# Gates and branch outputs of a hybrid decoder trunk as tokens x 512 channels, with the merged sums transposed

## The chip, the cores and the metric

The kernel runs on one core of a Trainium2 chip. A core has a matrix engine (TensorE, in the rows PE, its weight loads PEld), a vector engine (VectorE, DVE), an activation engine (ScalarE, ACT), a general engine (GpSimd, POOL) and a queue engine (SyncE, SP) that issues the DMAs. The metric is the device time of one execution in microseconds, the median of three runs.

## The reference

Two layers run over 256 tokens of 1024 channels; each ends in a residual addition, and a last RMS norm follows. In a layer the normalised input `h` is projected to everything at once: queries, keys, values and gate logits of three attention branches (8 heads of 64 each, so 512 channels), an indexer, and 3 x 1024 merge logits.

```python
    oa = moba_attention(rope(qa), rope(ka), va).reshape(B, S, WIDTH) * jax.nn.silu(ga)
    ob = dsa_attention(rope(qb), rope(kb_), vb_, qi, ki, wi).reshape(B, S, WIDTH) * jax.nn.silu(gb)
    oc = forgetting_attention(qc, kc, vc, log_f).reshape(B, S, WIDTH) * jax.nn.silu(gc)
    y = jnp.einsum('nbsw,nwd->bsnd', jnp.stack([oa, ob, oc], axis=0), w_branch)
    gates = jax.nn.sigmoid(merge_logit).reshape(B, S, N_BRANCH, D_MODEL)
    merged = jnp.sum(gates * y, axis=2)
    return x + jnp.einsum('bsd,de->bse', merged, w_out)
```

With 256 tokens the first branch is plain causal attention. The second keeps, for each token, the 64 keys with the highest indexer score. The third adds a running sum of log forget gates to its scores.

## The kernel before, in words

All products are float32 to nearly full precision, made of three matmuls in the rounded type float32r: each operand is split into a high part (a rounded copy, made by ACT) and a low part (the difference, made by DVE), and high x high, high x low and low x high are added up. So a stage of 8 blocks of 128 input channels has 24 matmuls for each output tile.

Weights come by DMA in chunks into three `raw` buffers, and pieces of 128 x 1024 numbers are split into the rings `wh` and `wl` (6 slots each): ACT's copy at line 380 and DVE's subtraction at line 384. Activations stand transposed, channels on partitions: `hTh` and `hTl` are the parts of the normalised input, `og` those of the gated branch outputs.

There are two kinds of projection. `unit_b` loads 128 columns of weights into PE and streams all 256 tokens past them, so that its matmuls are 256 columns wide and its result is channels x tokens. `unit_a` loads 128 tokens and streams 512 weight columns, so that its result is tokens x 512 channels; values and the output projection use it. Both issue their matmuls at line 428 into one of three PSUM tiles `proj`.

Before the change the merge gates (`unit_m`, 8 blocks of 128 channels for each branch, two neighbours sharing the pieces) and the branch outputs (`unit_y`, likewise) are made as channels x tokens. ACT takes a tanh of the gate logits (line 900 into `acc` for branch 0, line 903 into `mth` for the others). DVE multiplies tanh plus one with the branch output (lines 929 and 934) and adds the second and third product to `acc` (line 936). The sums are then in the form that the output projection loads as its tokens, and `split_to` writes their two parts into the value buffers `V`, which are free by then (lines 418 and 419).

A planner written in the file sets the order of instructions. Operations are recorded with their costs by engine, dependences, buffers and a key (the number of the unit that they belong to); `Plan.run` then picks, again and again, the engine that can start soonest and on it the operation that can start first, the lower key among equals. Every engine runs its list in order. The units are numbered in the order in which the layer's code makes them: values, indexer and the first mixer with gates in between (`between`), the third branch's mixer with branch outputs, the second branch's mixer with branch outputs, then the last gates and branch outputs, then the output projection. A mixer makes query, key and gate of two pairs of heads at a time, and their attention (`attend`) has the key of the last key unit plus one. `select`, the choice of the 64 keys, is recorded behind the last indexer unit: eight rounds of the eight highest scores (lines 886 and 887) on DVE, with keys that grow by 2.

Of the kernel before, what the change touches and what calls it, by code (L numbers as in the profile page):

```python
# [15 lines left out]
S = 256  # L16
# [27 lines left out]
MTH = 8  # L44
NC1 = 8
DMA_KEY = (-95, -94, -85, -84)
HI_KEY = (-60, -48, -47, -46)
NB1 = 0
# [199 lines left out]
def hybrid_trunk(ctx, tc, x, norm_gain, w_in, forget_bias, w_branch, w_out, final_gain, consts, out):  # L248
# [71 lines left out]
    acc = pool.tile([128, KC, S], F32, name="acc")  # L320
# [21 lines left out]
    k_acc = [Tok() for _ in range(KC)]  # L342
# [113 lines left out]
    def unit_a2(name, gets, ah, al, ra):  # L456

        us = [unit(f"{name}{t}") for t in range(2)]
        ps = [Buf("proj") for _ in range(2)]
        for t, q in ((0, (0, 1, 2)), (1, (0, 1, 2)), (0, (3,)), (1, (3,))):  # L460
            unit_a(f"{name}{t}", gets, t, ah, al, ra, part=(us[t], ps[t], q))
        return list(zip(us, ps))

    def unit_a(name, gets, t, ah, al, ra, c=0, n=512, part=None):
        u, ps, q = part or (unit(name), Buf("proj"), range(4))
        o = lambda: T(ps)[:, :n].rearrange("p (b a) -> p b a", a=2)
        for i in q:
# [82 lines left out]
    def final_part(t, c, n, i, key, on_dve):  # L550

        a = acc.rearrange("p k c -> p (k c)")
        x, sq = xs[t][:, c:c + n], a[:, D + c:D + c + n]
# [8 lines left out]
        dve(lambda: DVE.tensor_tensor(x, x, a[:, c:c + n], op=ALU.mult), n, [k_fg], [kx], key + 0.5, "final",  # L562
# [333 lines left out]
    def unit_m(l, n, j, gates):  # L896
        c0 = COL["mg"] + n * D + (j // 2) * 256
        u, ps = unit_b(f"m{n}{j}", lambda k: win_b(l, c0, k), j % 2)
        if n == 0:
            act(lambda: ACT.activation(acc[:, j], T(ps)[:, :S], AF.Tanh, scale=0.5), S, True, [ps], [k_acc[j]], u, "mth")  # L900
            return
        th = gates[n, j] = Buf("mth")
        act(lambda: ACT.activation(T(th), T(ps)[:, :S], AF.Tanh, scale=0.5), S, True, [ps], [th], u, "mth")

    def merged(j):
        v = V[j // 4].rearrange("p t h c -> p (t h c)")
        i = j % 4
        return [v[:, (2 * i + p) * S:(2 * i + p + 1) * S] for p in range(2)]

    k_mg = [k_V[j // 4][j % 4] for j in range(KC)]  # L910

    def unit_y(l, n, j, oi, gates, rank):
        u = unit(f"y{n}{j}")
        p = wbr(l, n, j, u)
        ps = Buf("proj")
        gh, gl = og[oi]
        cs = slice((j % 2) * 128, (j % 2) * 128 + 128)
        o = lambda: T(ps)[:, :S].rearrange("p (b a) -> p b a", a=2)
        g = []
        for k in range(4):  # L920
            wh, wl = lambda k=k: p[0].v[:, k, cs], lambda k=k: p[1].v[:, k, cs]
            g += [(wh, lambda k=k: turns(gh[:, k]), [p[0], k_og[oi][0][k]]), (wh, lambda k=k: turns(gl[:, k]), [p[0], k_og[oi][1][k]]),
                  (wl, lambda k=k: turns(gh[:, k]), [p[1], k_og[oi][0][k]])]
        g = [g[i] for i in (0, 1, 3, 4, 2, 5, 6, 7, 9, 10, 8, 11)]
        for a in (0, 6):
            mm_ops(o, g[a:a + 6], t_mm(256), [ps], u, f"y{n}{j}", a == 0, a == 6, True)
        ac = acc[:, j]
        if rank == 0:
            dve(lambda: DVE.scalar_tensor_tensor(ac, ac, 1.0, T(ps)[:, :S], op0=ALU.add, op1=ALU.mult), S,
                [ps], [k_acc[j]], u, "y")  # L930
            return
        th = gates[n, j]
        t = th
        dve(lambda: DVE.scalar_tensor_tensor(T(t), T(t), 1.0, T(ps)[:, :S], op0=ALU.add, op1=ALU.mult), S,
            [ps], [t], u, "y")
        plan.op([("DVE", t_dve(S), lambda: DVE.tensor_tensor(ac, ac, T(t), op=ALU.add)),
                 ("POOL", t_pool(S), lambda: POOL.tensor_tensor(ac, ac, T(t), op=ALU.add))], [t], [k_acc[j]], u, 0.0, "y").port = True
        if rank == 2:
            h, lo = merged(j)
            kh, kl = k_mg[j]  # L940
            split_to(lambda: plain(h), lambda: plain(lo), lambda: tiles(ac), S, False, [k_acc[j]], kh, kl, u, 0.5, "mg")
# [32 lines left out]
    hA = (lambda k, t: hTh[:, k, t * 128:(t + 1) * 128], lambda k, t: hTl[:, k, t * 128:(t + 1) * 128])  # L974
    mA = (lambda k, t: merged(k)[0][:, t * 128:(t + 1) * 128], lambda k, t: merged(k)[1][:, t * 128:(t + 1) * 128])

    def v_units(l, m, vi):
        gets = [lambda k, i=i: rows_a("A", w_in, l, COL["v" + m], i, k) for i in range(4)]
        for t in range(2):
            ra = [lambda k, p=p, t=t: [k_hT[p][t][k]] for p in range(2)]  # L980
            u, ps = unit_a(f"v{m}{t}", gets, t, hA[0], hA[1], ra)
            v_out(ps, t, vi, [ps], u)
# [62 lines left out]
    def m_of(l, n, gates, js):  # L1045
        return [lambda j=j: unit_m(l, n, j, gates) for j in js]

    def y_of(l, n, oi, rank, gates, js):
        return [lambda j=j: unit_y(l, n, j, oi, gates, rank) for j in js]
# [12 lines left out]

    def alternate(a, b):
        r = []
        for i in range(0, max(len(a), len(b)), 2):
            r += a[i:i + 2] + b[i:i + 2]
# [5 lines left out]
    for l in range(L):  # L1072
# [15 lines left out]
        for f in between(first, m_of(l, 0, gates, range(8)) + m_of(l, 2, gates, range(NC1))):  # L1088
            f()
        v_units(l, "c", 1)  # L1090
        for f in between(mixer(l, "c", 1, 1), alternate(m_of(l, 2, gates, range(NC1, 8)), y_of(l, 0, 0, 0, gates, range(8)))):
            f()
        v_units(l, "b", 0)
        for f in between(mixer(l, "b", 0, 0), alternate(y_of(l, 2, 1, 1, gates, range(8)), m_of(l, 1, gates, range(NB1)))):
# [53 lines left out]
```

## Time and profile before

| What | Value |
|---|---|
| Median of 3 runs | 602.46 us (602.02 to 602.86) |
| Profiled execution | 602.07 us |
| Its span, first to last instruction | 600.3 us |
| PE, DVE, ACT busy | 590.1, 526.0, 386.1 us |
| Mean granted TensorE clock | 0.997 of the upper level, 2.4 GHz |
| Moved by DMA | 107.69 MB, 179 GB/s |

Busy times of one engine are unions of its instructions' spans. Matmuls overlap, so two starts tell how long one occupies PE, and its recorded length does not. A releaser is the instruction that ended a wait, as semaphores tell.

### The profile page before, as it was taken

To read this page: it belongs to the slowest core of one execution; us is meant where nothing else is said; L and a number is where in the kernel's file an instruction comes from. 1 tells how busy PE (TensorE), PEld (TensorE's weight loads), DVE (VectorE), ACT (ScalarE), POOL (GpSimd) and SP (SyncE) were. 2 spreads that over 40 slices of the span, in tenths; PEclk is the share of its full clock that TensorE was granted. 3 is DMA by queue.
4 is the path that set the end of the run, shared out by engine and by line. 5 is a ranking of instruction groups with operands and counts; after the bars stand their busy time and mean duration, and the time that the engine had idled before them with its cause. 6 is when DMAs were issued, how large, how long until landed. Compare 5 with 4: busy or idle time off the path is not lost.

```text
span 600.3 us, 13137 instructions
## 1 busy us (share of the span) xinstructions
PE 590.1 (98%) x5164; PEld 568.9 (95%) x5164; DVE 526.0 (88%) x1232; ACT 386.1 (64%) x758; POOL 91.2 (15%) x100
## 2 busy tenths in 40 slices
PE   9999999999999999999999999999999999999995
PEld 8999999999999999999889999999999999999985
DVE  6799999986998999969588899998889989998783
ACT  5785575775767666765587566746766674776541
POOL 1234102200000504000003221230000014310001
PEclk9999999999999999999999999999999999999998
DMA  8859264836572654465546854465565455535701
GB/s 288 276 173 321 73 211 125 296 111 213 170 246 73 211 176 141 141 213 210 162 144 208 261 162 140 143 214 190 164 207 188 130 176 174 176 94 193 278 36 70
DMA packets 94461, 107.69 MB, mean 179 GB/s; under 512 B 4400, under 2 KB 82496, under 8 KB 94400
## 3 DMA queue, kind: packets, MB, share of 16 engines
q1 hardware_dynamic: 94112, 106.47, 55.4%
q8 instruction: 40, 0.66, 0.4%
q10 hardware_dynamic: 288, 0.39, 0.2%
q14 instruction: 21, 0.17, 0.1%
HBM read 105.79 MB, written 1.06 MB: 178 GB/s over the span
## 4 chain that ended last, share of the span: by engine, by line
PE 71%; DVE 24%; issue 3%; ACT 2%; POOL 0%; POOLq 0%; ACTq 0%
PE proj L428 62%; DVE wl L384 9%; PE d L609 2%; PE proj L1023 2%; DVE isc L887 2%; DVE e L683 1%; DVE t L886 1%; DVE rsh L483 1%; PE d L620 1%; DVE ptl L713 1%; DVE e L697 1%; DVE isc L865 1%; PE d L948 1%; ACT wh L380 1%; DVE rr L485 1%
## 5 line engine op out<-in xcount | busy, mean ns | idle before, releaser
L384 DVE TENSOR_TENSOR wl<-raw,wh 128x1024 fp32r<-128x1024 f32 (+1 forms) x190 | 240.3, 1282 | 27.5 <-ACT wh L380 22.6
L428 PE MATMUL proj<-hTh,wh 128*128 128x256 f32 (+1 forms) x1040 | 247.1, 277 | 0.0
L428 PE MATMUL proj<-hTl,wh 128*128 128x256 f32 (+1 forms) x1040 | 245.8, 276 | 0.0
L380 ACT ACTIVATE wh<-raw 128x1024 fp32r<-128x1024 f32 (+1 forms) x190 | 197.6, 1054 | 72.9 <-PE proj L428 40.2
L428 PEld LDWEIGHTS proj<-hTh,wh 128*128 128x128 f32 (+1 forms) x1040 | 199.0, 191 | 0.9
L428 PEld LDWEIGHTS proj<-hTl,wh 128*128 128x128 f32 (+1 forms) x1040 | 199.4, 192 | 0.2
L428 PE MATMUL proj<-hTh,wl 128*128 128x256 f32 (+1 forms) x1040 | 160.5, 277 | 0.6 <-DVE wl L384 0.6
L428 PEld LDWEIGHTS proj<-hTh,wl 128*128 128x128 f32 (+1 forms) x1040 | 136.8, 191 | 1.7 <-DVE wl L384 0.8
L484 POOL TENSOR_TENSOR rsh<-rsh,cst 128x256 f32<-128x256 f32 (+1 forms) x42 | 36.3, 866 | 314.8 <-DVE rsh L483 309.5
L687 ACT ACTIVATE e<-e,st 128x128 f32<-128x128 f32 x96 | 42.3, 442 | 17.7 <-DVE st L683 17.7
L486 POOL TENSOR_TENSOR rr<-rr,rsh 128x256 f32<-128x256 f32 (+1 forms) x42 | 46.7, 1116 | 10.1 <-DVE rr L485 5.6
L428 PE MATMUL proj<-wh,v 128*128 128x512 f32 (+1 forms) x144 | 33.7, 357 | 0.0
L428 PE MATMUL proj<-og0l,wh 128*128 128x256 f32 x128 | 31.9, 276 | 0.0
L428 PE MATMUL proj<-og0h,wh 128*128 128x256 f32 x128 | 31.9, 275 | 0.0
L428 PE MATMUL proj<-wh,hTl 128*128 128x512 f32 x80 | 30.6, 383 | 0.2 <-DVE hTl L546 0.2
L428 PE MATMUL proj<-wh,hTh 128*128 128x512 f32 x80 | 30.8, 385 | 0.0
L712 ACT ACTIVATE pth<-d 128x768 fp32r<-128x768 f32 x24 | 19.3, 803 | 17.0 <-PE o L726 15.0
L713 DVE TENSOR_TENSOR ptl<-d,pth 128x768 fp32r<-128x768 f32 x24 | 22.9, 952 | 7.7 <-ACT pth L712 7.6
L428 PEld LDWEIGHTS proj<-wh,v 128*128 128x128 f32 x144 | 25.3, 190 | 2.9
L428 PE MATMUL proj<-og0h,wl 128*128 128x256 f32 x128 | 24.8, 275 | 0.0
L428 PEld LDWEIGHTS proj<-og0l,wh 128*128 128x128 f32 x128 | 24.6, 192 | 0.0
L428 PEld LDWEIGHTS proj<-og0h,wh 128*128 128x128 f32 x128 | 24.6, 192 | 0.0
(190 smaller groups left out, 942.3 us busy)
## 6 DMA issues: line engine op xcount, KB each, us to landing
raw<-in_w_in_dram SPq DMA_DIRECT2D x74, 1024.0 KB, 5.3
raw<-in_w_branch_dram SPq DMA_DIRECT2D x24, 512.0 KB, 3.9
raw<-in_w_out_dram SPq DMA_DIRECT2D x8, 1024.0 KB, 5.8
brow<-drow SPq DMA_DIRECT2D x4, 512.0 KB, 6.5
raw<-in_w_in_dram SPq DMA_DIRECT2D x3, 512.0 KB, 6.4
x<-in_x_dram SPq DMA_DIRECT2D x4, 256.0 KB, 5.8
raw<-in_w_in_dram SPq DMA_DIRECT2D x2, 320.0 KB, 6.0
out_dram<-tmp SPq DMA_DIRECT2D x2, 320.0 KB, 2.5
```

The source lines that it names most:

```text
L380: ACT.activation(p[0].v, sel(c.v), AF.Copy)
L384: DVE.tensor_tensor(p[1].v, sel(c.v), p[0].v.bitcast(F32), op=ALU.subtract)
L428: PE.matmul(o(), a(), b(), start=first and i == 0, stop=last and i == n - 1)
L483: dve(lambda: DVE.stream_shuffle(T(sh)[:np_], a(), SWAP), S, [ps], [sh], key, "rope", t_dve(S) + 6.0)
L484: gps(lambda: POOL.tensor_tensor(T(sh)[:np_], T(sh)[:np_], s[:np_], op=ALU.mult), S, [k_rope], [sh], key, "rope")
L486: gps(lambda: POOL.tensor_tensor(T(r)[:np_], T(r)[:np_], T(sh)[:np_], op=ALU.add), S, [sh], [r], key, "rope")
L609: PE.matmul(T(d)[:, c:c + n].rearrange("p (b a) -> p b a", a=2), st[r, sl], turns(mv[r, :n]), start=i == 0, stop=i == 2, skip_group_check= ...
L687: act(lambda t=t, a=a, n=n, e=e, st=st: ACT.activation(T(e)[:, a:a + n], T(e)[:, a:a + n], AF.Exp, bias=T(st)[:, t:t + 1], scale=-1.0, acc ...
L712: act(lambda src=src, dst=dst: ACT.activation(dst(ph), src(), AF.Copy), 128 * n, True, [ps], k[:1], key, "pT", touch=[ph] + ps.banks)
L713: dve(lambda src=src, dst=dst: DVE.tensor_tensor(dst(pl), src(), dst(ph).bitcast(F32), op=ALU.subtract), 128 * n, [ps, k[0]], k[1:], key, ...
L887: dve(lambda o=o, t8=t8: DVE.match_replace(o, T(t8), o, TAKEN), n, [t8], [k_isc[i]], key + r * step, "top8")
L1023: PE.matmul(T(ps[t]).rearrange("p (b a) -> p b a", a=2), h(2 * i + x, t), turns(v3(w)[:, x]), start=left[t][0] == 23, stop=left[t][0] == 0)
```

## The change

Gates and branch outputs become units of the second kind: tokens x 512 channels, with one half of the channels (`hh`) and both token tiles in one unit, whose pieces of weights serve both tiles in turn. `unit_a2` takes the order of (token tile, pieces) as a list. Tanh, multiply and add work on 512 columns. The merged sums are then tokens x channels and have to be turned for the output projection: four transposes on PE for each half and token tile, from `acc` into a `d` tile of PSUM, from which ACT writes the high part and DVE the low part. The last branch's additions go to DVE alone; the others may go to POOL. Branch matrices are loaded in chunks of 512 columns. A mixer makes query, gate, key in this order, `select` begins 17 unit numbers later, and `between` hands out its units singly.

```diff
-MTH = 8
-NC1 = 8
+MTH = 4
+HC = (0, 1)
+O_ORDER = ((0, (0, 1)), (1, (0, 1)), (0, (2, 3)), (1, (2, 3)))
+M_ORDER = ((0, (0, 1)), (1, (0, 1)), (0, (2, 3)), (1, (2, 3)))
...
-    def wbr(l, n, j, k):
-        src = w_branch[l][n][:, (j // 2) * 256:(j // 2 + 1) * 256].rearrange("(k p) c -> p k c", p=128)
-        return piece(("Y", l, n, j // 2), ("Y", l, n, j // 2), src, [4, 256], lambda r: r, [4, 256], k)
+    def wbr(l, n, hh, i, k):
+        src = w_branch[l][n][:, hh * 512:(hh + 1) * 512].rearrange("(k p) c -> p k c", p=128)
+        return piece(("Y", l, n, hh, i), ("Y", l, n, hh), src, [4, 512], lambda r: r[:, 2 * i:2 * i + 2, :], [2, 512], k)
...
+    def unit_a2(name, gets, ah, al, ra, order, same=False):
+
+        n = len(gets)
         us = [unit(f"{name}{t}") for t in range(2)]
+        if n == 4:
+            unit(name)
         ps = [Buf("proj") for _ in range(2)]
-        for t, q in ((0, (0, 1, 2)), (1, (0, 1, 2)), (0, (3,)), (1, (3,))):
-            unit_a(f"{name}{t}", gets, t, ah, al, ra, part=(us[t], ps[t], q))
+        for t, q in order:
+            unit_a(f"{name}{t}", gets, t, ah, al, ra, part=(us[0] if same else us[t], ps[t], q))
         return list(zip(us, ps))
...
+    def units_m(l, n, hh, gates):
+        gets = [lambda k, i=i: rows_a("M", w_in, l, COL["mg"] + n * D + hh * W, i, k) for i in range(4)]
+        for t, (u, ps) in enumerate(unit_a2(f"m{n}{hh}", gets, hA[0], hA[1], rH, M_ORDER)):
+            if n == 0:
+                v, k = (lambda t=t: acc[:, t, hh * W:(hh + 1) * W]), k_acc[hh][t]
+            else:
+                k = gates[n, hh, t] = Buf("mth")
+                v = lambda k=k: T(k)
+            act(lambda v=v, ps=ps: ACT.activation(plain(v()), tiles(T(ps)), AF.Tanh, scale=0.5), W, True, [ps], [k], u, "mth")
...
+    def units_y(l, n, hh, oi, gates, rank):
...
+        for t, (u, ps) in enumerate(unit_a2(f"y{n}{hh}", gets, gA[0], gA[1], rG, ((0, (0, 1)), (1, (0, 1))))):
+            ac, ka = acc[:, t, hh * W:(hh + 1) * W], k_acc[hh][t]
+            if rank == 0:
+                dve(lambda ac=ac, ps=ps: DVE.scalar_tensor_tensor(plain(ac), plain(ac), 1.0, tiles(T(ps)), op0=ALU.add, op1=ALU.mult), W,
+                    [ps], [ka], u, "y")
+                continue
+            th = gates[n, hh, t]
+            dve(lambda th=th, ps=ps: DVE.scalar_tensor_tensor(plain(T(th)), plain(T(th)), 1.0, tiles(T(ps)), op0=ALU.add, op1=ALU.mult), W,
+                [ps], [th], u, "y")
+            ways = [("DVE", t_dve(W), lambda ac=ac, th=th: DVE.tensor_tensor(ac, ac, T(th), op=ALU.add)),
+                    ("POOL", t_pool(W), lambda ac=ac, th=th: POOL.tensor_tensor(ac, ac, T(th), op=ALU.add))]
+            plan.op(ways[:1] if rank == 2 else ways, [th], [ka], u, 0.0, "y").port = True
+            if rank < 2:
+                continue
+            at, kt = [d, d.banks[t]], Tok()
+
+            def tr(ac=ac, t=t, d=d):
+                for j in range(4):
+                    PE.transpose(T(d)[:, t * 512 + j * 128:t * 512 + (j + 1) * 128], ac[:, j * 128:(j + 1) * 128], ident)
+            pe(tr, 480.0, [ka, k_id], [kt], u, "mgT", MARGIN, touch=at)
...
+            act(lambda h=h, src=src: ACT.activation(h, src(), AF.Copy, scale=0.5), W, True, [kt], wh, u, "mg", touch=at)
+            dve(lambda h=h, lo=lo, src=src: DVE.scalar_tensor_tensor(lo, src(), 0.5, h.bitcast(F32), op0=ALU.mult, op1=ALU.subtract), W,
+                [kt] + wh, wl, u, "mg", t_dve(W) + 10.0, touch=at)
...
-                for hf in range(2) for kind in "qkg" for p in (2 * hf, 2 * hf + 1)]
+                for hf in range(2) for kind in "qgk" for p in (2 * hf, 2 * hf + 1)]
...
-                select(u + 3, 2.0)
+                select(u + 20, 2.0)
```

At the end of the first layer, on PE, the branch outputs of the last branch (from `og0h`) run into the output projection (from `v0` and `v1`, where the merged sums stand). Before:

```order
L428 MATMUL proj1_165<-og0h_95,wh4_67 128x256
L428 MATMUL proj1_165<-og0l_96,wh4_67 128x256
L428 MATMUL proj1_165<-og0h_95,wh4_67 128x256
L428 MATMUL proj1_165<-og0l_96,wh4_67 128x256
L428 MATMUL proj1_165<-og0h_95,wl4_74 128x256 x2
L428 MATMUL proj0_164<-wh5_68,v0_84 128x512 x4
L428 MATMUL proj0_164<-wl5_75,v0_84 128x512 x2
L428 MATMUL proj0_164<-wh0_63,v0_84 128x512 x4
L428 MATMUL proj0_164<-wl0_70,v0_84 128x512 x2
L428 MATMUL proj0_164<-wh1_64,v1_85 128x512 x4
```

Now, at the same place, from the second transpose of the layer on (line 941 turns `acc` into `d`):

```order
L941 MATMUL d1_164<-cst_109,acc_114 128x128 x4
L429 MATMUL proj1_161<-wh4_67,og0h_95 128x512
L429 MATMUL proj1_161<-wh4_67,og0l_96 128x512
L429 MATMUL proj1_161<-wh4_67,og0h_95 128x512
L429 MATMUL proj1_161<-wh4_67,og0l_96 128x512
L429 MATMUL proj1_161<-wl4_74,og0h_95 128x512 x2
L941 MATMUL d0_163<-cst_109,acc_114 128x128 x4
L429 MATMUL proj2_162<-wh5_68,v0_84 128x512 x4
L429 MATMUL proj2_162<-wl5_75,v0_84 128x512 x2
L429 MATMUL proj2_162<-wh0_63,v0_84 128x512 x4
L429 MATMUL proj2_162<-wl0_70,v0_84 128x512 x2
L429 MATMUL proj0_160<-wh5_68,v0_84 128x512 x4
```

Blocks of four transposes stand between the matmuls now, and the wide matmuls take the outputs as their loaded side.

On DVE at the same place, the multiplies (`mth` with `proj`), adds (`acc`), splits of merged sums (`v0`) and weight subtractions (`wl`). Before:

```order
L934 SCALAR_TENSOR_TENSOR mth0_156<-mth0_156,proj2_166 128x256
L936 TENSOR_TENSOR acc_114<-acc_114,mth0_156 128x256
L934 SCALAR_TENSOR_TENSOR mth1_157<-mth1_157,proj1_165 128x256
L936 TENSOR_TENSOR acc_114<-acc_114,mth1_157 128x256
L384 TENSOR_TENSOR wl1_71<-raw1_124,wh1_64 128x1024
L419 SCALAR_TENSOR_TENSOR v0_84<-acc_114,v0_84 128x256 x2
```

Now, from the first multiply of the last branch on:

```order
L930 SCALAR_TENSOR_TENSOR mth0_156<-mth0_156,proj1_161 128x512
L932 TENSOR_TENSOR acc_114<-acc_114,mth0_156 128x512
L385 TENSOR_TENSOR wl1_71<-raw1_124,wh1_64 128x1024
L930 SCALAR_TENSOR_TENSOR mth1_157<-mth1_157,proj2_162 128x512
L385 TENSOR_TENSOR wl2_72<-raw1_124,wh2_65 128x1024
L947 SCALAR_TENSOR_TENSOR v0_84<-d1_164,v0_84 128x4x128
L932 TENSOR_TENSOR acc_114<-acc_114,mth1_157 128x512
L930 SCALAR_TENSOR_TENSOR mth2_158<-mth2_158,proj0_160 128x512
```

The split reads the transposed sums from `d1`, and two weight subtractions and a split now stand ahead of the second add.

On DVE in the first layer's first mixer, the rounds of the selection (MAX and MATCH_REPLACE on `isc`), the low parts of the keys (`k1l`, `k2l`) and the weights. Before:

```order
L886 MAX t80_152<-isc_115 128x8
L886 MAX t81_153<-isc_115 128x8
L887 MATCH_REPLACE isc_115<-t80_152,isc_115 128x128
L887 MATCH_REPLACE isc_115<-t81_153,isc_115 128x256
L886 MAX t82_154<-isc_115 128x8
L886 MAX t83_155<-isc_115 128x8
L415 TENSOR_TENSOR k1l_102<-rr1_129,k1h_101 128x256
L415 TENSOR_TENSOR k2l_104<-rr0_128,k2h_103 128x256
L384 TENSOR_TENSOR wl3_73<-raw2_125,wh3_66 128x1024
```

Now, around the same two keys:

```order
L385 TENSOR_TENSOR wl3_73<-raw2_125,wh3_66 128x1024
L488 STREAM_SHUFFLE rsh0_126<-proj1_161 128x256
L416 TENSOR_TENSOR k1l_102<-rr1_129,k1h_101 128x256
L490 TENSOR_TENSOR rr0_128<-proj1_161,cst_109 128x256
L890 MAX t83_155<-isc_115 128x8
L894 TENSOR_SCALAR selb_116<-isc_115 128x128
L891 MATCH_REPLACE isc_115<-t83_155,isc_115 128x256
```

Weights and a key's rotation stand between the selection's rounds, whose last one comes behind the first key's low part.

## Rows read from the trace of the kernel before

**Rows 1.** The page: span and busy times.

```profile
span 600.3 us, 13137 instructions
PE 590.1 (98%) x5164; PEld 568.9 (95%) x5164; DVE 526.0 (88%) x1232; ACT 386.1 (64%) x758; POOL 91.2 (15%) x100
```

**Rows 2.** The timeline of PE from 300 to 319 us: start, length, instruction. Rows with a count hold several merged instructions; between the first two rows from 310.65 lie twelve matmuls, as between the next two and the last two.

```profile
300.36 1.04 PE L532 MATMUL d<-cst,tmp 128*128 128x128 f32 x8
301.15 0.46 PE L428 MATMUL proj<-wh,v 128*128 128x512 f32 x1
...
310.65 0.38 PE L428 MATMUL proj<-wh,hTh 128*128 128x512 f32 x1
...
313.24 0.38 PE L428 MATMUL proj<-wh,hTh 128*128 128x512 f32 x1
...
314.53 0.27 PE L428 MATMUL proj<-hTh,wh 128*80 128x256 f32 x1
...
315.84 0.27 PE L428 MATMUL proj<-hTh,wh 128*80 128x256 f32 x1
...
317.15 0.28 PE L428 MATMUL proj<-hTh,wh 128*128 128x256 f32 x1
...
318.49 0.28 PE L428 MATMUL proj<-hTh,wh 128*128 128x256 f32 x1
```

**Rows 3.** The waits of PE over the whole span: who waited for whom, us in total, times, longest. The rows left out are those of the program's start and of the normalisation between the layers.

```profile
PE o L725 <- DVE ot L743: 0.9, 2, 0.4
PE proj L428 <- DVE wl L384: 0.6, 1, 0.6
PE d L609 <- DVE k1l L415: 0.5, 1, 0.5
...
PE o L727 <- DVE ptl L713: 0.2, 1, 0.2
```

**Rows 4.** The timeline of PE at the five waits of the steady part, each time the instruction before the wait and the one behind it, with its idle time and releaser in brackets.

```profile
72.55 0.28 PE L609 MATMUL d<-k1h,ql 64*128 64x256 f32 x2
73.36 0.38 PE L609 MATMUL d<-k1l,qh 64*128 64x256 f32 x2 [0.54 <-DVE k1l L415]
...
91.79 0.22 PE L726 MATMUL o<-pth,v 128*128 128x128 f32 x1
92.25 0.27 PE L727 MATMUL o<-ptl,v 128*64 128x128 f32 x1 [0.24 <-DVE ptl L713]
...
233.03 0.39 PE L428 MATMUL proj<-og1h,wl 128*128 128x256 f32 x2
233.83 0.35 PE L725 MATMUL o<-pth,v 128*128 128x256 f32 x1 [0.41 <-DVE ot L743]
...
391.22 0.28 PE L428 MATMUL proj<-hTl,wh 128*128 128x256 f32 x1
392.14 0.71 PE L428 MATMUL proj<-hTh,wl 128*128 128x256 f32 x4 [0.65 <-DVE wl L384]
...
525.01 0.39 PE L428 MATMUL proj<-og1h,wl 128*128 128x256 f32 x2
525.84 0.35 PE L725 MATMUL o<-pth,v 128*128 128x256 f32 x1 [0.45 <-DVE ot L743]
```

**Rows 5.** Stretches of the span: from and to, length, busy time (and instructions) of PE, PEld, DVE, ACT and POOL, granted clock, busy share of the DMA engines, GB/s.

```profile
22.00:93.00 71.00, 70.23 (x668) 68.86 (x667) 68.09 (x182) 48.97 (x95) 19.78 (x20) 1.00 0.63 201
...
214.00:258.00 44.00, 43.59 (x445) 42.68 (x444) 43.45 (x117) 32.37 (x72) 8.52 (x9) 1.00 0.54 169
258.00:298.00 40.00, 40.00 (x287) 37.91 (x287) 29.29 (x46) 21.52 (x34) 0.00 (x0) 1.00 0.63 206
...
506.00:550.00 44.00, 43.55 (x444) 42.64 (x444) 43.24 (x116) 32.38 (x72) 8.53 (x9) 1.00 0.54 168
550.00:589.00 39.00, 39.00 (x284) 37.10 (x284) 27.61 (x45) 19.63 (x32) 0.00 (x0) 1.00 0.38 136
```

**Rows 6.** Transposes of 128 x 128 in the trace of before: a piece of the chain of waits (start, us, what), and the group of all 32 by line and shape (busy us, mean ns of one, idle before).

```profile
14.91 0.44 PE d L532 x4
...
L532 PE MATMUL d<-cst,tmp 128*128 128x128 f32 x32 | 4.3, 273 | 0.0
```

**Rows 7.** Groups of instructions by line and shape: engine, operation, operands, count, busy us, mean ns of one, idle time before them and what ended it.

```profile
L384 DVE TENSOR_TENSOR wl<-raw,wh 128x1024 fp32r<-128x1024 f32 x188 | 238.8, 1287 | 27.5 <-ACT wh L380 22.6 <-ACT tmp L854 2.2 <-PE proj L428 0.5
L486 POOL TENSOR_TENSOR rr<-rr,rsh 128x256 f32<-128x256 f32 x40 | 45.3, 1136 | 9.9 <-DVE rr L485 5.6 <-ACT wh L380 2.0
L934 DVE SCALAR_TENSOR_TENSOR mth<-mth,proj 128x256 f32<-128x256 f32 x32 | 12.9, 414 | 0.3 <-PE proj L428 0.2
L936 DVE TENSOR_TENSOR acc<-acc,mth 128x256 f32<-128x256 f32 x32 | 12.8, 422 | 0.2
L903 ACT ACTIVATE mth<-proj 128x256 f32<-128x256 f32 x32 | 12.0, 374 | 6.0 <-PE proj L428 5.9
L418 ACT ACTIVATE v<-acc 128x256 fp32r<-128x256 f32 x16 | 7.4, 497 | 3.0 <-DVE acc L936 3.0
L988 ACT ACTIVATE v<-proj 128x512 fp32r<-128x512 f32 x12 | 7.1, 595 | 3.5 <-PE proj L1023 2.8 <-PE proj L428 0.5
L419 DVE SCALAR_TENSOR_TENSOR v<-acc,v 128x256 fp32r<-128x256 f32 x16 | 6.8, 458 | 0.0
L1113 DVE TENSOR_TENSOR x<-x,proj 128x512 f32<-128x512 f32 x7 | 4.8, 686 | 7.5 <-PE proj L428 7.4
```

More of the change, by code (lines that the diff above doesn't have):

```diff
@@ L319, in hybrid_trunk @@
     tmp6 = pool.tile([128, 1536], F32, name="tmp6")
-    acc = pool.tile([128, KC, S], F32, name="acc")
+    acc = pool.tile([128, 2, D], F32, name="acc")
     isc = pool.tile([128, 384], F32, name="isc")
@@ L341, in hybrid_trunk @@
     k_og = [[[Tok() for _ in range(4)] for _ in range(2)] for _ in range(2)]
-    k_acc = [Tok() for _ in range(KC)]
+    k_acc = [[Tok() for _ in range(2)] for _ in range(2)]
     tag("raw", R_RAW, [128, 2048])
@@ L561, in final_part @@
                 key, "norm sq", 93.0)
-        dve(lambda: DVE.tensor_tensor(x, x, a[:, c:c + n], op=ALU.mult), n, [k_fg], [kx], key + 0.5, "final",
+        dve(lambda: DVE.tensor_tensor(x, x, acc[:, 0, c:c + n], op=ALU.mult), n, [k_fg], [kx], key + 0.5, "final",
             port=True)
@@ L905, in merged @@
[L905 to L941, printed above, removed]
@@ L979, in v_units @@
         for t in range(2):
-            ra = [lambda k, p=p, t=t: [k_hT[p][t][k]] for p in range(2)]
-            u, ps = unit_a(f"v{m}{t}", gets, t, hA[0], hA[1], ra)
+            u, ps = unit_a(f"v{m}{t}", gets, t, hA[0], hA[1], rH)
             v_out(ps, t, vi, [ps], u)
@@ L1042, in mixer, with m_of, y_of @@
         return [lambda kind=kind, p=p: pair_unit(l, m, prs[p], kind, p)
-                for hf in range(2) for kind in "qkg" for p in (2 * hf, 2 * hf + 1)]
[L1045 to L1049, printed above, removed]
+                for hf in range(2) for kind in "qgk" for p in (2 * hf, 2 * hf + 1)]
+    def m_of(l, n, gates, hs=(0, 1)):
+        return [lambda hh=hh: units_m(l, n, hh, gates) for hh in hs]
+    def y_of(l, n, oi, rank, gates):
+        return [lambda hh=hh: units_y(l, n, hh, oi, gates, rank) for hh in range(2)]
     def between(main, fill, first=0):
         main = [main[i:i + 2] for i in range(0, len(main), 2)]
-        fill = [fill[i:i + 2] for i in range(0, len(fill), 2)]
         r, n = [], len(main) - first
@@ L1058, in between @@
             if i >= first:
-                for g in fill[(i - first) * len(fill) // n:(i - first + 1) * len(fill) // n]:
-                    r += g
+                r += fill[(i - first) * len(fill) // n:(i - first + 1) * len(fill) // n]
         return r
@@ L1064, in alternate @@
         r = []
-        for i in range(0, max(len(a), len(b)), 2):
-            r += a[i:i + 2] + b[i:i + 2]
+        for i in range(max(len(a), len(b))):
+            r += a[i:i + 1] + b[i:i + 1]
         return r
@@ L1085, in index_unit @@
             if p == 3:
[L1086 removed]
+                select(u + 20, 2.0)
         first = [lambda p=p: index_unit(p) for p in range(4)] + mixer(l, "a", 0, 0)
[L1088 removed]
+        for f in between(first, m_of(l, 0, gates) + m_of(l, 2, gates, HC)):
             f()
         v_units(l, "c", 1)
[L1091 removed]
+        for f in between(mixer(l, "c", 1, 1), alternate(m_of(l, 2, gates, [h for h in range(2) if h not in HC]), y_of(l, 0, 0, 0, gates))):
             f()
         v_units(l, "b", 0)
[L1094 removed]
+        for f in between(mixer(l, "b", 0, 0), y_of(l, 2, 1, 1, gates)):
             f()
[L1096 removed]
+        for f in m_of(l, 1, gates) + y_of(l, 1, 0, 2, gates):
             f()
```

49 lines of the change are left out of this document (24 added, 25 removed).

## The prediction

> **What bounds the kernel now.** Read first the busy line [rows 1]: PE is busy for 98% of 600.3 us, DVE for 88%, ACT for 64%; the granted clock is 1.00 in every stretch of rows 5, which is the upper level. A busy PE is not yet a PE at its pace, since its matmuls overlap, so read next how far apart they start [rows 2]. From 310.65 to 313.24 lie twelve matmuls of 512 columns: 2.59 us, 215.8 ns each. From 317.15 to 318.49 lie twelve of 256 columns: 1.34 us, 111.7 ns each. Third, look for places where two starts lie further apart than that. PE's waits are few [rows 3], and the five places behind them in the steady part of the program [rows 4] lose: at 72.55, 0.81 less a pace of 0.11 is 0.70; at 91.79, 0.46 less 0.06 is 0.40; from 233.03 two matmuls take 0.80 in place of 0.22, 0.58; at 391.22, 0.92 less 0.11 is 0.81; from 525.01, 0.83 less 0.22 is 0.61. Together 3.10 us. In all five the thing waited for is made by DVE. Last, the stretches [rows 5]: DVE is busy for 68.09 of 71 us in the first, and for all but half a microsecond or so in the two 44 us stretches, while it rests in the last 40 us of each layer (29.29 and 27.61 busy). So TensorE's own work bounds nearly everything; DVE keeps up in the crowded stretches with little to spare. The tail behind 589 and the start are not touched by the change.
>
> **The sum is made against the profiled execution**, 602.07 us: a span of 600.3 and 1.77 around it. It lies 0.39 under the median of 602.46.
>
> **Wider matmuls.** The gates were 3 x 8 units of 24 matmuls per layer, the branch outputs 3 x 8 of 12: 864 per layer, 1728 in all, of 256 columns. They become 864 of 512 with the same products. 1728 x 0.1117 = 193.0 us; 864 x 0.2158 = 186.5. That is 6.5 us less, all on the path, since PE has no idle cover.
> The Trainium skill ("TensorE: Matmul & The Clock Gate", Back-to-back issue gap) gives one matmul its columns over the clock and a small fixed part, by which 512 columns cost 215.8 ns and 256 cost about 109.2. The trace agrees on the first and not on the second [rows 2]; by the page's figure this term would be 2.2 us, which the fourth rival comes to as well.
>
> **Transposes.** 4 per half and token tile, 16 per layer, 32 in all, 128 x 128 in float32. The same form stands in the trace: four take 0.44 us on the chain of waits, eight 0.79 from 300.36 to the next matmul's start at 301.15 [rows 2, 6], so 0.10 to 0.11 each. 32 x 0.11 = 3.5 us on PE, again on the path. One alone is recorded at 273 ns [rows 6], but the next starts before it ends; were all 32 paid in full it would be 8.7 us. I take 3.5, since blocks of four are what is added.
> PE's balance is 6.5 - 3.5 = 3.0 us less.
>
> **What DVE and ACT gain.** DVE multiplied 48 times at 0.42 (19.9 us), added 32 times at 0.42 (13.5), and split 16 times at 0.46 (7.3) [rows 7]: 40.7 us. Now it multiplies 24 times 512, adds 12 (four more adds are POOL's), splits 8 times: 44 instructions. A 512-column operation of that kind is 0.686 [rows 7], so 30.2. DVE has some 10 us less of its 526. ACT's 48 tanhs (18.0 us) become 24 at 0.595 (14.3), its 16 copies (8.0) become 8 (4.8); ACT is off the path, and its 7 us are worth nothing by themselves. The four adds on POOL are of 512 columns; POOL's sum of 256 is 1.14 us [rows 7], so about 2.3 each by twice the width, beside DVE, and none is the last add before a transpose. I count nothing.
> What DVE's relief is worth is bounded by the 3.10 us of lost starts above it, and by nothing below. The selection of keys moves from right behind the index scores to 17 unit numbers later, so that its top-8 steps no longer stand in one block before a key's low part: before, the last steps of the block end where the score matmuls wait 0.70 us at 72.55 [rows 4]. But there the order now puts other steps of the selection and a shuffle behind the weights, in front of the second key's low part, and one wait can return. I take 1.2 of the 3.1.
>
> **What the transposes' waits cost.** A gate-times-output tile is multiplied and added on DVE (0.69 + 0.69), and only then can PE transpose it. Behind the waiting transpose stand the next branch or output matmuls, whose data is ready; behind it in data stand ACT's copy (0.60), DVE's split (0.69) and the output projection's matmuls on that half. The order gives each transpose cover. The first of a layer has 12 matmuls between its tile's last matmul and itself, 2.6 us, against 1.4 of DVE. The second has 4 transposes and 18 matmuls, 4.3 us; in that time DVE does two weight subtractions (1.29 each), a multiply, a split and an add, 2 x 1.29 + 3 x 0.69 = 4.6 us, of which part of the first subtraction can start earlier. So there, once per layer, it is level: 0 to 0.7 us. The third has 12 + 4 in front, the last 4 transposes and 18 matmuls, 4.3 us, against 1.4 of its own chain and what DVE has queued. The first output matmul on the second half follows the third transpose after 24 matmuls and 4 transposes, 5.6 us, and the first that needs the fourth follows it after 18 matmuls, 3.9 us, each against 1.3 of copy and split. I take 0.25 us per layer, 0.5 in all. The low bound is 0; the high one is one weight subtraction late at each of the eight, 8 x 1.29 = 10.3.
>
> **The rest at nothing.** Loads of weights: the same bytes, the branch matrices in 12 loads of 1 MB in place of 24 of 512 KB, and gate weights in rows twice as wide. The DMA engines are 0.38 to 0.63 busy in the stretches behind 22 us [rows 5], and no wait of PE in rows 3 names a load; if that cover went, one late piece of weights would stall PE by the 0.8 us at 391.22 [rows 4]. Weight pieces: as many as before (8 per gate, 4 per branch), so 188 subtractions of 1.29 us stay. The gates' buffers: four of 512 in place of eight of 256, the same room; they come free in larger steps, which costs at most one tanh (0.6) where the next gate is early. A gate unit now holds two of the three accumulators for 48 x 0.2158 = 10.4 us; the third must carry queries, gates and keys meanwhile, whose evacuation takes two DVE steps of 0.42 against 2.7 us of matmuls per unit. Query, gate, key: the same instructions, with the gate's tanh out of the way when scores begin; 0, and no more either way than one wait for keys of 0.70 us at each of the twelve blocks of scores.
>
> **Sum.** 602.07 - 6.5 + 3.5 - 1.2 + 0.5 = 598.4, and 0.39 more for the median: 598.7 us.
>
> **Rivals.**
> *More of the lost starts go.* With DVE 10 us lighter all five places close and the transposes never wait: 602.46 - 3.0 - 3.1 = 596.4. For it: all five name DVE. Against it: the two at 233.03 and 525.01 are waits for the single accumulator of the values product, which the order spaces much as before.
> *The gain is eaten by coarser filling.* Gate work now comes in pieces of 10.4 us where it came in 5.4, so that attention steps in the crowded stretches find less to lie behind; one more stall of 0.7 in each of the two crowded parts of either layer is 2.8 us, with no relief elsewhere: 602.46 - 3.0 + 2.8 = 602.3. For it: the accumulators are three. Against it: the selection is no longer one block in the first of these parts, and DVE's multiplies and adds in the second are fewer.
> *The transposes stop PE.* PE runs in order, so a transpose whose add is late stops ready matmuls. From 0.53 us at each of the eight (4.2 us in all, the 3.0 and the 1.2) the change is slower than before; with one weight subtraction late at each it ends at 602.46 - 3.0 + 10.3 = 609.8. For it: DVE's load is level with its cover at one of the four per layer. Against it: DVE is 29 of 40 us busy in that part before the change [rows 5].
> *Width saves less.* With 80 columns of weights, twelve matmuls of 256 take 1.31 us from 314.53 to 315.84, 109.2 ns each [rows 2]. If the 2.5 ns above that belong to what is queued beside these units and follow the work into its wide form, the saving is 864 x 2.6 ns = 2.2 us, and with 3.5 for the transposes the time 603.8. Against it: the wide form was seen at 215.8 with 128 columns of weights.
> *Transposes paid in full.* At 273 ns each, 8.7 us, the balance is 2.2 us more, 604.7. Against it: the next start after one is 109 ns later.
> The Trainium skill (TensorE: Matmul & The Clock Gate, PE-mode transpose) reports about 275 ns for a transpose within a kernel. The recorded length agrees with 273 [rows 6], and the pace does not.
>
> **How the numbers follow.** Forecast 0.60, the larger gain 0.18, eaten gain 0.13, stopped PE 0.06, less by width 0.02, full transposes 0.01. By itself the forecast reaches from 597 to 600.9: below, the transposes at 0.10 and 2.6 of 3.1; above, no relief of DVE and 0.7 at the level transposes. The range takes in the larger gain and most of the eaten one: 595.8 to 602.0. A change within 0.2%, 1.2 us, cannot be told from none here. Faster: 0.60 + 0.18 = 0.78; the same 0.13; slower 0.06 + 0.02 + 0.01 = 0.09.
>
> **What would show it.** In the profile after: starts of the gates' matmuls 215.8 apart; 32 transposes in blocks of about 0.44; DVE's busy time near 515; PE's waits on the sources of rows 3 still about 2 us, with a new group for the transposes under 0.6. It is wrong if the transposes wait for adds by more than that, if PE's waits in the crowded stretches grow, or if the last 40 us of a layer get longer.

## The result, and the profile after

The kernel after takes 599.15 us (median of 4 runs, 598.86 to 599.43), the kernel before 602.24 beside it. The ratio is 0.9948, with a 95% interval of 0.9936 to 0.9961: 3.1 us faster, 0.45 above the forecast. The profiled execution took 598.98 us.

The first lines of the page, against [rows 1]:

```profile
span 597.1 us, 11359 instructions
PE 587.2 (98%) x4332; PEld 538.2 (90%) x4332; DVE 516.8 (87%) x1164; ACT 387.0 (65%) x736; POOL 100.2 (17%) x110
```

PE has 832 matmuls fewer and is busy for the same 98%. DVE is busy for 9.2 us less, near the 10 that were forecast, but only in part for the reason given. The recorded lengths of multiplies, adds and splits fell from 40.7 to 30.0 us, as forecast. Records of successive DVE instructions overlap, though, and by what each adds to the busy time these groups went from 33.9 to 27.6, 6.3 less. The weight subtractions gave 5.4 where nothing was counted: the same 188 take 32 ns less each [rows 7]. All other work on DVE takes 2.5 more. The rows of the subtractions, and of multiplies and adds:

```profile
L385 DVE TENSOR_TENSOR wl<-raw,wh 128x1024 fp32r<-128x1024 f32 x188 | 233.6, 1255 | 26.3 <-ACT wh L381 23.2 <-PE o L732 0.8 <-PE proj L429 0.4
L930 DVE SCALAR_TENSOR_TENSOR mth<-mth,proj 128x512 f32<-128x512 f32 x16 | 10.8, 678 | 1.4 <-PE proj L429 1.4
L932 DVE TENSOR_TENSOR acc<-acc,mth 128x512 f32<-128x512 f32 x12 | 8.3, 688 | 0.3
L933 POOL TENSOR_TENSOR acc<-acc,mth 128x512 f32<-128x512 f32 x4 | 7.0, 1742 | 17.4 <-DVE mth L930 17.4
```

The stretches of [rows 5] again (length, busy us of PE, PEld, DVE, ACT, POOL, granted clock, DMA share, GB/s):

```profile
22.00:93.00 71.00, 70.45 (x529) 64.96 (x529) 67.94 (x183) 44.05 (x79) 20.13 (x22) 1.00 0.62 206
214.00:258.00 44.00, 43.97 (x359) 40.11 (x358) 43.26 (x103) 32.34 (x71) 13.15 (x12) 1.00 0.48 162
258.00:298.00 40.00, 40.00 (x200) 35.15 (x199) 28.43 (x40) 20.54 (x30) 1.36 (x2) 1.00 0.55 176
```

The gates' matmuls start 215.8 ns apart, as forecast: twelve of them lie between the two rows from the timeline of PE.

```profile
262.88 0.38 PE L429 MATMUL proj<-wh,hTl 128*128 128x512 f32 x1
...
265.47 0.38 PE L429 MATMUL proj<-wh,hTl 128*128 128x512 f32 x1
```

The end of a layer, where the transposes are, has PE busy throughout, and DVE still rests. The crowded stretches are as crowded as before: 67.94 of 71 us.

What PE waited for (sum, times, longest), against [rows 3]; the waits at the program's start and at the change of layers are left out:

```profile
PE o L731 <- DVE ptl L717: 1.3, 2, 1.0
...
PE proj L429 <- DVE wl L385: 0.3, 1, 0.3
...
PE d L613 <- DVE k2l L416: 0.2, 1, 0.2
PE d L624 <- DVE e L701: 0.2, 1, 0.2
```

No wait stands at the transposes, but the sum for DVE is what it was, at other places. Two of them, on the timeline of PE, and the product that came too late at the first, on those of DVE and ACT (`pth` and `ptl` are the high and the low part of the attention weights, which the product with the values reads):

```profile
99.19 0.22 PE L730 MATMUL o<-pth,v 128*128 128x128 f32 x1
100.37 0.27 PE L731 MATMUL o<-ptl,v 128*64 128x128 f32 x1 [0.96 <-DVE ptl L717]
...
390.24 0.22 PE L730 MATMUL o<-pth,v 128*128 128x128 f32 x1
390.79 0.27 PE L731 MATMUL o<-ptl,v 128*64 128x128 f32 x1 [0.33 <-DVE ptl L717]
```

```profile
97.09 2.36 DVE L385 TENSOR_TENSOR wl<-raw,wh 128x1024 fp32r<-128x1024 f32 x2
99.37 0.95 DVE L717 TENSOR_TENSOR ptl<-d,pth 128x768 fp32r<-128x768 f32 x1
...
97.90 0.80 ACT L716 ACTIVATE pth<-d 128x768 fp32r<-128x768 f32 x1
```

The high part, pth, was there at 98.70 (ACT's copy, 0.80 from 97.90), but DVE had begun a second weight subtraction, so ptl started at 99.37 and PE stood for 1.18 less a pace of 0.06.

For all kernels below, one count is made from the records of the matmuls: the interval between two successive starts, less the pace of the first (0.216, 0.112, 0.062 and 0.038 us for 512, 256, 128 and 64 columns; 0.109 for a transpose), wherever more than 0.18 us is left, from 20 us on. It is called **lost starts**. Before has 3.62 (the five of [rows 4] and 0.53 at the change of layers, which every kernel has), after 3.99. The kernel before ran beside each of the others, and its medians there lie between 602.10 and 602.45 us; a few tenths between the medians of two kernels therefore say little by themselves.

### The profile page after: what moved, and what is told of

Same layout as the page of the kernel before. It is cut to its first block, busy times and chain, and to the rows that moved or that the text cites. A ratio compares the mean times of both kernels' runs of the same rounds, so it can differ in the third digit from the quotient of the medians.

```text
span 597.1 us, 11359 instructions
## 1 busy us (share of the span) xinstructions
PE 587.2 (98%) x4332; PEld 538.2 (90%) x4332; DVE 516.8 (87%) x1164; ACT 387.0 (65%) x736; POOL 100.2 (17%) x110
## 4 chain that ended last, share of the span: by engine, by line
PE 85%; DVE 10%; issue 2%; ACT 1%; DMA 1%; POOL 0%; POOLq 0%; DVEq 0%
PE proj L429 74%; PE d L613 4%; DVE wl L385 3%; PE proj L1027 2%; PE d L624 2%; PE o L732 1%; PE o L729 1%; DVE isc L891 1%; DVE t L890 1%; PE o L731 1%; PE d L941 1%; DVE rsh L488 1%; DMA x<-in_x_dram 1%; PE o L730 0%; ACT wh L381 0%
## 5 line engine op out<-in xcount | busy, mean ns | idle before, releaser
L429 PE MATMUL proj<-hTh,wh 128*128 128x256 f32 (+1 forms) x656 | 155.6, 276 | 0.0
L429 PE MATMUL proj<-hTl,wh 128*128 128x256 f32 (+1 forms) x656 | 154.9, 275 | 0.0
L429 PEld LDWEIGHTS proj<-hTh,wh 128*128 128x128 f32 (+1 forms) x656 | 125.2, 191 | 0.6
L429 PEld LDWEIGHTS proj<-hTl,wh 128*128 128x128 f32 (+1 forms) x656 | 125.2, 191 | 0.3
L429 PE MATMUL proj<-wh,hTh 128*128 128x512 f32 x272 | 105.1, 386 | 0.0
L429 PE MATMUL proj<-wh,hTl 128*128 128x512 f32 x272 | 103.3, 380 | 0.2 <-DVE hTl L551 0.2
L429 PE MATMUL proj<-hTh,wl 128*128 128x256 f32 (+1 forms) x656 | 100.4, 276 | 0.0
L429 PE MATMUL proj<-wl,hTh 128*128 128x512 f32 x272 | 81.0, 379 | 0.3 <-DVE wl L385 0.3
L429 PEld LDWEIGHTS proj<-wh,hTl 128*128 128x128 f32 x272 | 51.5, 189 | 7.5 <-DVE hTl L551 1.2
L429 PEld LDWEIGHTS proj<-wh,hTh 128*128 128x128 f32 x272 | 51.4, 189 | 7.5
```

What stands on the lines that cost most here:

```text
L429: PE.matmul(o(), a(), b(), start=first and i == 0, stop=last and i == n - 1)
```

## The experiments

**Width.** The kernel after with the wide matmuls cut in two, in the order of after.

```
+ halves = 2 if name[0] in "my" else 1
...
+ for h in range(halves):
+     cs = slice(h * 128, (h + 1) * 128) if halves == 2 else slice(None)
+     PE.matmul(o()[:, cs], a(), b()[:, cs], ...)
```

> The kernel after, with each of the 864 matmuls of gates and branch outputs issued as two of 256 columns into the two halves of the same tile; all engines' order stays, only PE gets 864 more matmuls. Theory (width is what gained): 864 x (2 x 111.7 - 215.8) ns = +6.6 us on 599.2, so 605.7 us, a ratio to the kernel before of 1.006. Rival 'width saves less' (a narrow matmul at 109.2 ns): 864 x 2.6 ns = +2.2 us, 601.4 us, ratio 0.999. Rival 'the gain came from the new order, not from width': under +1 us, below 600.2 us, ratio under 0.997.

The mark that begins a sum (`start`) stands on both halves here, and the sums of gates and branch outputs aren't the reference's; in the two later kernels with halves it stands on the first alone, and they are. Measured: 603.59 us, ratio 1.0024 (1.0015 to 1.0033), 4.4 us more than after. All three theories miss. The pace is as expected: halves start 111.7 ns apart (twelve between the two rows of PE below). What was left out is that a slower PE waits less: lost starts fall from 3.99 to 2.33. 6.6 - 1.7 = 4.9, against 4.7 in the spans (601.8 and 597.1) and 4.4 in the medians; 0.2 to 0.5 is left over. The profile of this kernel has only the last row left of the waits on ptl, k2l and e:

```profile
264.79 0.39 PE L432 MATMUL proj<-wh,hTl 128*128 128x256 f32 x2
...
266.13 0.39 PE L432 MATMUL proj<-wh,hTl 128*128 128x256 f32 x2
...
PE o L735 <- DVE ptl L721: 0.8, 2, 0.6
```

**Transposes.** Each is issued twice.

```
- for j in range(4):
+ for j in (0, 1, 2, 3, 0, 1, 2, 3):
      PE.transpose(...)
```

> The kernel after, with each of the 32 transposes of the merged sums issued a second time into the same place, right behind the four of its block. Theory (a transpose costs PE its pace of 109 ns): 32 x 0.109 = +3.5 us, so 602.7 us, ratio 1.001. Rival (it costs its recorded length of 273 ns): +8.7 us, 607.9 us, ratio 1.009. Rival (it lies in time that PE would have lost anyway): under +0.5 us, ratio under 0.996.

Measured: 602.89 us, ratio 1.0012 (1.0004 to 1.0021): 3.7 us more, near the 3.5 of the pace of 109 ns and far from its rivals; lost starts are 4.37, 0.4 more. The timelines of PE, of after and then of this kernel, show a block: 0.36 to the next start, against 0.79 with four more.

```profile
273.02 0.60 PE L941 MATMUL d<-cst,acc 128*128 128x128 f32 x4
273.38 0.46 PE L429 MATMUL proj<-wh,og0h 128*128 128x512 f32 x1
273.68 0.38 PE L429 MATMUL proj<-wh,og0l 128*128 128x512 f32 x1
```

```profile
273.63 1.04 PE L941 MATMUL d<-cst,acc 128*128 128x128 f32 x8
274.42 0.46 PE L429 MATMUL proj<-wh,og0h 128*128 128x512 f32 x1
274.72 0.38 PE L429 MATMUL proj<-wh,og0l 128*128 128x512 f32 x1
```

The matmul behind a block is followed after 0.30 instead of 0.216; with that, a block of four costs 0.44, and the eight blocks of after 3.5.

**DVE's load.** Multiplies and adds of 512 columns in two, then in four instructions.

```
- DVE.scalar_tensor_tensor(plain(ac), plain(ac), 1.0, tiles(T(ps)), ...)
+ for h in range(2):
+     o = plain(v)[:, h:h + 1]
+     DVE.scalar_tensor_tensor(o, o, 1.0, tiles(T(ps))[:, h:h + 1], ...)
```

> The kernel after, with the 24 multiplies and the 12 adds of 512 columns on DVE each issued as two of 256 columns: by the rows of before and after 24 x (2 x 414 - 678) + 12 x (2 x 422 - 688) ns = +5.5 us of DVE, which takes DVE's relief of this change away, PE's instructions and order unchanged. Theory (the relief of DVE was worth nothing, the waits only changed places): within 0.5 us of 599.2, ratio 0.994 to 0.996. Rival (the relief was worth the 1.2 us that the prediction counted, and something else lost as much): +1.2 us or more, 600.4 us, ratio 0.997 or above.

> The kernel after, with the multiplies and adds of 512 columns on DVE each issued as four of 128: 108 instructions more, by the halves (36 more, 2.1 us more of DVE's busy time) some 58 ns each, so DVE +6.3 us, two thirds of its relief of 9.2 us; PE unchanged. Theory B (PE loses starts by how closely DVE has to follow it; the 6.6 us that narrow matmuls added to PE took 1.9 us of lost starts away, 0.29 us for each): +1.8 us, 601.0 us, ratio 0.998. Theory A (the lost starts sit at a few places where weight subtractions were put first, whatever DVE's load): under +0.5 us, ratio under 0.9957.

Measured: 599.62 us, ratio 0.9957 (0.9944 to 0.9971), with DVE busy for 518.9; and 600.41, ratio 0.9966 (0.9953 to 0.9979), with 523.2. The halves cost DVE 2.1 us and not 5.5, since their records of 410 ns overlap. For 2.1 and 6.4 us more of DVE, PE loses 0.5 and 1.3: lost starts are 4.46 and 5.34. That lies between the theories (A under 0.5, B 1.8), nearer to B: load costs, some 0.2 us for each. The intervals of both ratios overlap that of after, so it is the lost starts that carry this reading. The first run by itself would have borne out its theory that the load is worth nothing; it takes the second to see the cost. There the waits name four ptl instead of two. The other two were late in after as well, by 0.2 each (at 230.5 and 520.5), and now lose 0.66 and 0.65:

```profile
PE o L731 <- DVE ptl L717: 2.3, 4, 1.0
```

> Both at once: matmuls of gates and branch outputs in halves of 256 columns, and the multiplies and adds on DVE in quarters, so that PE has its old pace and DVE two thirds of its old load back. With halves alone 603.6 us. Theory B (load against pace): about +1.8 us on that, 605.4 us, ratio 1.0054. Theory A (places alone): under +0.5 us on that, ratio under 1.0033. If PE's slower pace gives DVE so much room that its load no longer matters, also under +0.5 us here, but above +1 us without the halves.

Measured: 604.58 us, ratio 1.0039 (1.0027 to 1.0051), 1.0 us above halves alone; lost starts 3.10 against 2.33. The load costs somewhat less at the slower pace, but the difference between 1.3 and 1.0 is within the intervals, so neither theory is confirmed.

**The order.** Two edits of order in the change can be undone by themselves: the units' (query, gate, key) and the selection's. The new turns of the output projection (`O_ORDER`) and of `between` have no run of their own. First, both of them in the kernel before; then both undone in the kernel after; then one undone at a time.

```
- ... for kind in "qkg" ...
+ ... for kind in "qgk" ...
...
- select(u + 3, 2.0)
+ select(u + 20, 2.0)
```

> The kernel before with the two edits of order alone: units query, gate, key, and the selection at key u + 20. Theory (the order of the units is worth nothing by itself; what the change gains is PE's work): within 0.7 us of 602.2, ratio 0.999 to 1.001. Rival (the order is what closed the waits of before): -1.2 us or more, ratio 0.998 or below. Rival (it was tuned for the wide tiles and costs the old kernel something): +1.2 us or more, ratio 1.002 or above.

> The kernel after with the two edits of order undone: units query, key, gate, and the selection at key u + 3. Theory (order is worth nothing by itself): within 0.7 us of 599.2, ratio 0.9937 to 0.9960. Rival (the order hides the coarser filling of the wide tiles): +1.2 us or more, ratio 0.9968 or above. Rival (the new order is what opened the waits of after): -1.2 us or more, ratio 0.9928 or below.

> The kernel after with units query, key, gate as before, but the selection at u + 20 as after. Theory (the gates ahead of the keys are what opened waits on ptl in after; the late selection is a gain, since with the early one DVE put MAX8 and MATCH_REPLACE8 ahead of a product that frees a tile for PE, 1.1 us lost at 65.0): 1.0 us below both edits undone, 596.6 us, ratio 0.990 to 0.991. Rival (the late selection is worth nothing, units are all): 597.6 us, ratio 0.992. Rival (the late selection is what cost 1.5 us): 599.2 us, ratio 0.9945 or above.

> The kernel after with units query, gate, key as after, but the selection at u + 3 as before. Theory (units make the difference): 599.2 us or up to 1 us more, ratio 0.9945 to 0.9965. Rival (the late selection cost 1.5 us): 597.6 us, ratio 0.992 to 0.9928.

Measured: order alone 607.1 us (median of 606.67 to 609.49, a wide scatter that lifts the ratio), ratio 1.0086 (1.0073 to 1.01), so 4.7 us slower than before by the medians. Both undone 597.64, ratio 0.992 (0.9908 to 0.9933), which is faster than before and after. The four combinations in the wide kernel, us and lost starts:

| units | selection at u + 3 | at u + 20 |
|---|---|---|
| query, key, gate | 597.64, 2.48 | 600.94, 5.48 |
| query, gate, key | 598.69, 3.59 | 599.15, 3.99 |

Ratios of the two mixed ones: 0.9978 (0.9969 to 0.9987) with the old units, 0.9942 (0.9929 to 0.9954) with the old selection. The expectation for the former, that the late selection is a gain, falls: it costs 3.3 us there, and 0.5 with the new units (the latter within the intervals). The other lies just under the edge that the theory of the units gave (0.9945), and far from its rival. The two edits aren't independent: with the late selection the new units gain 1.8 us, with the early one they cost 1.1. In the kernel before, where the two edits cost 4.7 us, lost starts go from 3.62 to 7.34, and this is what the waits show, with a product of the rotation and a ptl ahead:

```profile
PE proj L428 <- DVE rr L485: 1.8, 1, 1.8
PE o L727 <- DVE ptl L713: 1.2, 1, 1.2
...
PE proj L428 <- DVE g L654: 0.9, 2, 0.5
```

With both undone, the wide kernel has no wait on ptl, k2l or e left; the largest now is one of 1.1 us on a product of the rotation, at 65.0. Its first ptl comes behind two weight subtractions as in after, but PE gets there later (timelines of DVE and of PE in this kernel):

```profile
82.60 2.35 DVE L385 TENSOR_TENSOR wl<-raw,wh 128x1024 fp32r<-128x1024 f32 x2
84.87 0.95 DVE L717 TENSOR_TENSOR ptl<-d,pth 128x768 fp32r<-128x768 f32 x1
```

```profile
86.51 0.22 PE L730 MATMUL o<-pth,v 128*128 128x128 f32 x1
86.57 0.22 PE L731 MATMUL o<-ptl,v 128*64 128x128 f32 x1
```

ptl ends at 85.82, 0.75 before PE needs it; in after it ended when PE had stood for a microsecond.

**The order at the slower pace.** Both edits undone, and the halves of the first experiment.

> The kernel after with both edits of order undone (597.6 us) and the matmuls of gates and branch outputs issued in halves of 256 columns: +6.6 us of PE. Theory (a slower PE takes back only the waits for DVE that there are: 1.9 us in the new order, where PE waits for ptl, k2l and e; in the old order there is one of 1.1 us at 65.0 and one of 0.5 at 39.3): +5.0 to +6.6 us, 602.6 to 604.2 us, ratio 1.0003 to 1.003. Rival (a slower PE gives 1.9 us back whatever the order): 602.3 us, ratio below 1.0. Together with the new order in halves (603.6 us) it gives what the order is worth at the narrow pace: under the theory less than 1 us, against 1.5 us at the wide pace and 4.9 us in the kernel before.

Measured: 603.32 us, ratio 1.0017 (1.0008 to 1.0026), 5.7 above both undone: inside what the theory gave, outside the rival. Lost starts go from 2.48 to 1.95, so 0.5 came back where the new order gave 1.7. At the narrow pace the order is worth 0.3 us (603.59 and 603.32, within the intervals), at the wide pace 1.5. A slow pace alone doesn't make order harmless, though: the kernel before runs at the narrow pace too and lost 4.7 by the same edits. What makes it more sensitive, its heavier load on DVE or its other tiles, no run tells.

**Two attempts at the waits.** In after, the planner is made to put ptl ahead of whatever could start up to 0.5 us before it.

```
+ ... touch=[ph, pl] + ps.banks).rush = 500.0
...
- cand.append((bw[0], o.key, o.n, o, bw[1]))
+ cand.append((bw[0], o.key - (1000.0 if o.rush else 0.0), o.n, o, bw[1]))
...
- ... if c[4][0] == e and c[0] <= lim)
+ ... if c[4][0] == e and c[0] <= lim + c[3].rush)
```

> The kernel after, with one rule more in the planner: the subtraction that makes ptl (L717) goes on DVE ahead of everything else that could start up to 0.5 us before it, the weight subtractions above all; same instructions, another order. Theory (the largest lost starts of after, 1.1 us at 99.2, 0.5 at 390.2, 0.2 at 230.5 and at 520.5 us, are weight subtractions that were put before a ptl that PE waits for): -1 to -2 us, 597.2 to 598.2 us, ratio 0.992. Rival (removed waits come back at another place, as they did from before to after): within 0.5 us of 599.2, ratio 0.994 to 0.996. Rival (weight pieces come late because DVE idles for ptl): +0.5 us or more, ratio above 0.996.

Measured: 601.76 us, ratio 0.9992 (0.9983 to 1.0001), 2.6 us worse than after. The wait at 390 is gone, the one at 99 is still there (1.11), and the outputs' low part has become late at the end of either layer; lost starts are 6.22. The waits of this kernel:

```profile
PE proj L430 <- DVE og0l L417: 1.7, 2, 1.2
...
PE o L732 <- DVE ptl L718: 1.0, 1, 1.0
```

Then a third buffer for the rotation's products, on top of both edits undone, for that one large wait, which the timeline of PE shows:

```profile
64.81 0.59 PE L429 MATMUL proj<-wl,hTh 128*128 128x512 f32 x2
66.38 0.48 PE L429 MATMUL proj<-wh,hTh 128*128 128x512 f32 x1 [0.97 <-DVE rr L490]
```

```
- ("rr", 2, S, F32)
+ ("rr", 3, S, F32)
```

> The kernel after with both edits of order undone (597.6 us) and a third buffer for the products rr of the rotation (2 to 3), since the one large lost start left there, 1.1 us at 65.0, is PE waiting for a tile that the product rr (L490) reads, and that product ran only after the subtraction that read the buffer it needs. Theory (that wait goes and nothing else comes): -1.1 us, 596.5 us, ratio 0.990. Rival (a new plan brings waits elsewhere, as in the two other new orders tried): 597.6 us or more, ratio 0.992 or above.

Measured: 597.87 us, ratio 0.9927 (0.9913 to 0.9941): no gain. The wait on rr is gone, and two on ptl have come (waits of this kernel); lost starts are 2.90 against 2.48.

```profile
PE o L731 <- DVE ptl L717: 0.8, 2, 0.6
```

## Why the prediction was right, and where it was not

**Wider matmuls, 6.5.** Right. Gates and branch outputs start 215.8 ns apart, and cutting them again puts 6.6 us of matmuls back; the rival of the smaller saving falls.

**Transposes, 3.5.** Right, by the block of 0.44 and by the doubling, which cost 3.7 with 0.4 more of lost starts in it. In full (273 ns each) it would have been 8.7.

**DVE's relief, 1.2 of 3.1.** The size came out, but as a net of several things, and the places were others. With both edits of order undone, the lost starts of [rows 4] go from 3.10 to 1.95 (2.48 less the 0.53 of the layers), 1.15 less. In the same order at the old pace they'd be 1.42 (1.95 of the kernel with halves and both edits undone, less the 0.53): so 1.7 less, of which the faster PE takes 0.5 back. Of DVE's 10 us, the multiplies, adds and splits gave 6.3. That the relief alone made the 1.7 isn't shown: DVE's load was put back only in the new order, where it cost 0.2 us for each us. The step put part of its 1.2 to the later selection; that cost 3.3 us with the old units and nothing clear of the noise with the new, and in neither order did it gain. In after as it stands the relief is gone: 3.46, without the layers' 0.53. The step did name the risk that a wait would return on the second key's low part (the row on k2l is that one).

**Query, gate, key: 0.** This step failed, and the selection's move with it. Together they cost the wide kernel 1.5 us, and 4.7 in the kernel before. The bounds set for it held; the 0 did not, because the same instructions in another order meet DVE's queue at other points.

**The transposes' waits, 0.5.** They were 0: no row of waits names the transposes. The forecast's sum was -3.7 and the medians moved by -3.1; a cost of order, 1.5, was missing, and this wait, 0.5, was counted and didn't come, so that by luck the total erred by less than the steps. By the runs it reads: -6.6 for width, +3.5 for transposes, -1.2 for lost starts in the old order, +1.5 for the new order, -2.8 in all; the other 0.3 is not assigned to a step.

**Missing altogether** was the link between PE's pace and the waits. The halves show it: of 6.6 us put on PE, 1.7 came back from waits for DVE in the new order, 0.5 in the old. So here a gain on PE was paid out less what DVE couldn't follow.

**The rivals.** The coarser filling was to bring waits of 0.7 in the crowded parts; after has such waits, but with both edits of order undone the same wide tiles have none on ptl, k2l or e, and one of 1.1 at 65.0 in their place, so the width of the filling alone doesn't make them. Stopped or fully paid transposes fall. The larger gain (596.4, all five places closed) was not reached by any kernel; 597.64 is the nearest.

## What to carry to other kernels

Where one engine is busy for 98% and the next for 87%, look whether the second can follow before you book a saving on the first, and count the matmuls' starts, not the busy share. An edit of order that rides along with a change of size belongs in a run of its own, since two such edits were worth from -1.8 to +3.3 us here by the company they were in, and cost 1.5 of the 4.8 us that the rest of the change gained. Closing a single wait by hand in a planned order opened others in both attempts here; the sum over all lost starts says whether anything was won.

## What was not expected of the hardware

Cutting 36 DVE operations of 678 to 688 ns in two cost 2.1 us, 58 ns a cut, though the halves are recorded at 410 ns each: successive records on DVE overlap, and the sum of recorded lengths overstates what a cut costs. The 188 weight subtractions became 32 ns shorter each (1287 to 1255) with no change to them. The traces tell where: subtractions during which POOL does nothing last 1.22 us in either kernel, and those that a POOL operation overlaps last 1.57 before (35 of them) and 1.43 after (33), which makes 5.3 us of the 6.0 that they gained together. Two subtractions from the timeline of DVE in after, the first beside POOL's work, the second with POOL at rest, and the two operations of POOL ahead of them:

```profile
228.10 1.74 DVE L385 TENSOR_TENSOR wl<-raw,wh 128x1024 fp32r<-128x1024 f32 x1
230.96 1.21 DVE L385 TENSOR_TENSOR wl<-raw,wh 128x1024 fp32r<-128x1024 f32 x1
...
226.17 1.72 POOL L489 TENSOR_TENSOR rsh<-rsh,cst 128x256 f32<-128x256 f32 x1
227.96 0.79 POOL L491 TENSOR_TENSOR rr<-rr,rsh 128x256 f32<-128x256 f32 x1
```

That POOL's work is the cause no run shows by itself, since none moves it alone. And a transpose recorded at 272 to 273 ns took 109 of PE's time also when eight stood in a row, at a granted clock of 1.00.
